# Channel mixers whose up panels keep tokens stationary, with results turned in 32x32 blocks

## The chip, the cores and the metric

The kernel runs on one core of one Trainium2 chip. A core has TensorE (PE in the profile) for matrix products, VectorE (DVE), ScalarE (ACT), GpSimd (POOL) and SyncE (SP), which only issues transfers, and 16 DMA engines. PE takes a stationary operand of 128x128 from SBUF, streams up to 512 columns of a moving operand past it and adds the product into a PSUM bank. The metric is the device time of one execution in microseconds, the median over runs.

## The reference

A decoder trunk of two layers works on 256 tokens of width 2048 in fp32. Each layer is a mixer (gated linear attention in the first, forgetting attention in the second, both with four heads of attention to 256 memory tokens) and then a channel mixer. The change touches only the channel mixer:

```python
def causal_dwconv(u, w, b):
    s_ = u.shape[1]
    up = jnp.pad(u, ((0, 0), (CONV_WIDTH - 1, 0), (0, 0)))
    return w[0] * up[:, 0:s_] + w[1] * up[:, 1:s_ + 1] + w[2] * up[:, 2:s_ + 2] + b

def conv_ffn(h, w_up, conv_w, conv_b, w_down):
    u = causal_dwconv(h @ w_up, conv_w, conv_b)
    a, val = split_cols(u, [FFN_HIDDEN, FFN_HIDDEN])
    return (jax.nn.silu(a) * val) @ w_down
...
h = rmsnorm(x, norm_ffn[i])
x = x + conv_ffn(h, ffn_w_up[i], ffn_conv_w[i], ffn_conv_b[i], ffn_w_down[i])
```

The hidden width is 5632, so `w_up` has 11264 columns (gate, then value). The convolution runs over the tokens, with three taps and a bias for each column.

## The kernel before, in words

**Numbers in halves.** PE works on `float32r`. Each fp32 operand is kept as a high half (a copy rounded to that type) and a low half (what the copy lost), and a product is three products: high by high, high by low, low by high. An activation buffer (`bufA`, `bufB`) is 16 tiles of 128 features x 2 halves x 256 tokens, features on the partitions. A norm's gain is folded into the halves; its factor for each token (`row()`) is multiplied in after the projection.

**Weights.** All weights lie in memory as a row of units of 1024 columns x 128 partitions (512 KB), in the order of use (`_panels`, `_layout`). `split_unit` (L189) loads a unit through SyncE (L200), makes the high half on ACT (L205) and the low half on DVE (L206). There are four buffers each for the raw unit, the high half and the low half. These instructions are traced with a priority 300 instructions ahead, so that they run as early as the buffers allow.

**Two forms of a projection.** With weights stationary (`proj_fm`, `panels_fm`, L240 and L242), a panel of 256 columns takes four units. For each chunk of 128 features and each 128 columns there is one matmul of 512 moving columns (high weights, both halves of the 256 tokens) and one of 256 (low weights, high tokens). Results come out with features on the partitions, as two partial sums that `whole` (L249) adds: a copy on ACT (L252) and an addition on DVE (L254). With tokens stationary (`proj_tm` L286, `panel_tm` L311), a panel of up to 512 columns takes eight units of two chunks. For each chunk and each block of 128 tokens there are three matmuls whose moving operand is the weights. Results come out with tokens on the partitions, already summed in PSUM.

**The channel mixer** (`ffn`, L1023). The 44 blocks of 128 hidden columns are done in three parts of 16, 16 and 12 (`PARTS`). For each part, all its up panels run first, then four down panels of 512 output columns that contract over the blocks of that part; the result is added to the residual `x` (L322). An up panel holds 128 gate and the matching 128 value columns, weights stationary. `up_out` brings each half of it through `whole`, multiplies by the norm's row (L1038), applies the convolution (ACT L1042 for one tap and the bias, DVE L1043 and L1044 for the others), then silu (L1047), the product (L1048) and the split into halves in `m` (L352, L353). The first three up panels of a layer are interleaved by `three_fm` so that their last units, which need the last four feature chunks of `h`, come late.

**Turning.** Where the residual has to become features on partitions for the next stage (`preparing`, L1062), DVE turns it in 32x32 blocks (L1077), and `move` (L462, L466) sends the blocks between partition groups by 16 DMAs of 32 KB on SyncE. `split_turned` then reads the moved tile (L363, L365).

**Order of the work.** A scheduler orders each engine's instructions when the program is built, by priority and by its own estimate of when they can start. The order on each engine is then fixed, and waits are by semaphore. `issue_after` holds instructions behind a given one on its engine. SyncE issues in order too: a load or move that must wait holds up those behind it.

**PSUM.** Eight banks: four for accumulators (`pacc`), and in `pwork` two under the tag `s` and one each under `t` and `o`.

Of the kernel before, what the change touches and what calls it, by code (L numbers as in the profile page):

```python
# [12 lines left out]
F32 = mybir.dt.float32  # L13
# [6 lines left out]
P = 128  # L20
# [3 lines left out]
HID = 5632  # L24
# [30 lines left out]
def _panels():  # L55
# [5 lines left out]

    def fm(key, w, c0, kcs=full, second=None):
        cols = [(c0, 256)] if second is None else [(c0, 128), (second, 128)]
        out.append((key, w, kcs, cols, 4))

# [75 lines left out]
def _trunk(ctx: ExitStack, tc: tile.TileContext, xt, xtok, memt, wp, wgu, gns, gfin, cnv, par, msk, out):  # L141
# [39 lines left out]

    loads, casts, ends = [], [], []

# [5 lines left out]
    def split_unit(unit, pool=wpool, pieces=1, before=None):  # L189

        off, kcs, n = unit
        w = len(kcs) * n
        with tc.high_priority(offset=AHEAD):
            raw = wpool.tile([P, NUNIT], F32, name="raw", tag="raw", bufs=4)
            hi = pool.tile([P, NUNIT], F32R, name="whi", tag="whi", bufs=4 if pool is wpool else 3)
            lo = pool.tile([P, NUNIT], F32R, name="wlo", tag="wlo", bufs=4 if pool is wpool else 3)
            src = wp[off : off + P * w].rearrange("(p n) -> p n", p=P)
            for i in range(pieces):
                s = slice(i * w // pieces, (i + 1) * w // pieces)
                loads.append(nc.sync.dma_start(raw[:, s], src[:, s]))  # L200
            for i in range(pieces):
                s = slice(i * w // pieces, (i + 1) * w // pieces)
                if before is not None:
                    before(i)
                casts.append(S.activation(hi[:, s], raw[:, s], AF.Copy))  # L205
                V.tensor_tensor(lo[:, s], raw[:, s], hi[:, s].bitcast(F32), ALU.subtract)  # L206
        return hi, lo
# [84 lines left out]

    def panel_tm(key, src, evac):

# [22 lines left out]

        return step

    def add_to(f):  # L320
# [692 lines left out]

    def add_out(key, src, then=None, spare=None, last=None, first=0):
        for f in range(first, 4):
            def evac(b, a, f=f):
                add_to(f)(b, a)
                if then is not None:
                    then(f, b)

            proj_tm((*key, f), src, last if f == 3 and last is not None else evac, spare if f == 3 else None)

    def ffn(l, nx, h, m, then, spare=None, last=None):  # L1023
        with tc.tile_pool(name=f"ffn{l}", bufs=1) as fp:
# [5 lines left out]
            turn = [0]  # L1030
            for p, (lo, hi) in enumerate(PARTS):
                def up_out(j, i):
                    cv = {}

                    def evac(c, a):
                        u = us[turn[0] % 4]
                        turn[0] += 1
                        V.tensor_tensor(u[:, 2:], whole(a), nx.row(), ALU.mult)  # L1038
# [4 lines left out]
                        V.scalar_tensor_tensor(r, u[:, 1 : T + 1], w[1], r, ALU.mult, ALU.add)  # L1043
                        V.scalar_tensor_tensor(r, u[:, :T], w[0], r, ALU.mult, ALU.add)  # L1044
                        cv[c] = r
                        if c == 1:
                            S.activation(cv[0], cv[0], AF.Silu)  # L1047
                            V.tensor_tensor(r, cv[0], r, ALU.mult)  # L1048
                            split(m, i, r)

                    return evac

                first = 0
# [45 lines left out]
    with tc.tile_pool(name="stash", bufs=1) as st:  # L1099
# [4 lines left out]
        with tc.tile_pool(name="turn1", bufs=1) as tp:  # L1104
            n2, then = preparing("kv", bufB, tp, turned3, "mix1")
            ffn(0, n, bufB, bufA, then)
        fox(n2, vt, turned3)
# [9 lines left out]
    with tc.tile_pool(name="store", bufs=1) as op:  # L1117
# [41 lines left out]

        ffn(1, n, bufA, bufB, then, op, last)  # L1160

# [70 lines left out]
```

## Time and profile before

| what | value |
|---|---|
| median of 3 runs | 2263.23 us (2262.76 to 2263.59) |
| the profiled execution's own time | 2263.27 us |
| its span in the trace | 2261.4 us |
| PE busy | 2249.8 us, 99% |
| DVE busy | 1617.1 us, 72% |
| ACT busy | 1250.7 us, 55% |
| granted PE clock | 0.999 |
| HBM over the span | 192 GB/s |

Engines are busy beside one another. PE's matmuls overlap in the records, so the mean length of one record (390 ns for 512 columns) is longer than the distance from one matmul to the next. The distance has to be taken from stretches of many. A group's idle time is what its engine stood just before its instructions, with what ended the wait; it costs time only on an engine that sets the end. "SPq" rows are the issuing of a DMA by SyncE, not its transfer.

### The profile page before, as it was taken

How to read it: one execution, taken by the hardware profiler on the slowest of the kernel's cores; microseconds unless marked ns; L12 is line 12 of the kernel's file. 1: busy time of each engine (PE TensorE's matmuls, PEld its weight loads, DVE VectorE, ACT ScalarE, POOL GpSimd, SP SyncE). 2: the span in 40 equal slices, each digit the busy share in tenths (PEclk: the TensorE clock that was granted, in tenths of full speed). 3: DMA queues.
4: the chain of work that ended last, by engine and by line, in shares of the span. 5: the costliest groups of instructions: out<-in, count | busy, mean ns of one | idle time of the engine just before them, and what ended most of it. 6: DMA issues, size and time to landing. Idle time of an engine off the chain costs nothing.

```text
span 2261.4 us, 33526 instructions
## 1 busy us (share of the span) xinstructions
PE 2249.8 (99%) x12253; PEld 1967.1 (87%) x12253; DVE 1617.1 (72%) x2746; ACT 1250.7 (55%) x1986; POOL 3.4 (0%) x19
## 2 busy tenths in 40 slices
PE   9999999999999999999999999999999999999998
PEld 8889998888888888888888998888888888888887
DVE  7779877677765777557777569677776577756775
ACT  6657675555543555445555555456554455534554
POOL 0000000000000000000000000000000000000000
PEclk9999999999999999999999999999999999999999
DMA  9655554665555555555565567766656555655554
GB/s 341 198 184 166 177 168 171 214 201 190 191 196 189 190 193 188 195 188 192 189 217 202 183 192 240 229 204 218 194 189 198 188 189 191 192 194 187 191 193 147
DMA packets 142125, 444.38 MB, mean 197 GB/s; under 512 B 18428, under 2 KB 34952, under 8 KB 141832
## 3 DMA queue, kind: packets, MB, share of 16 engines
q1 hardware_dynamic: 140808, 441.05, 58.8%
q8 instruction: 96, 1.57, 0.3%
q10 hardware_dynamic: 1152, 1.19, 0.2%
q14 instruction: 69, 0.57, 0.1%
HBM read 429.31 MB, written 5.52 MB: 192 GB/s over the span
## 4 chain that ended last, share of the span: by engine, by line
PE 96%; ACT 1%; DVE 1%; DMA 1%; issue 0%; SPq 0%; DVEq 0%; ACTq 0%
PE acc L242 37%; PE acc L286 34%; PE acc L240 20%; PE acc L311 2%; PE ps_s L242 1%; PE ps_s L240 1%; DMA raw<-wp 0%; ACT whi L205 0%; DVE wlo L206 0%; PE ps_s L758 0%; PE ps_o L495 0%; PE ps_s L495 0%; PE ps_o L931 0%; PE ps_s L976 0%; ACT L822 0%
## 5 line engine op out<-in xcount | busy, mean ns | idle before, releaser
L206 DVE TENSOR_TENSOR wlo<-raw,whi 128x1024 fp32r<-128x1024 f32 (+4 forms) x809 | 968.7, 1201 | 518.5 <-ACT whi L205 429.9
L205 ACT ACTIVATE whi<-raw 128x1024 fp32r<-128x1024 f32 (+4 forms) x809 | 839.6, 1039 | 600.5 <-PE acc L286 311.2
L242 PE MATMUL acc<-B,whi 128*128 128x512 f32 x2048 | 482.6, 390 | 0.0
L242 PEld LDWEIGHTS acc<-B,whi 128*128 128x128 f32 x2048 | 378.9, 188 | 75.2
L286 PE MATMUL acc<-whi,mix 128*128 128x512 f32 x1216 | 302.5, 389 | 0.0
L242 PE MATMUL acc<-mix,whi 128*128 128x512 f32 x1224 | 298.3, 391 | 0.0
L286 PEld LDWEIGHTS acc<-whi,mix 128*128 128x128 f32 x1216 | 228.3, 188 | 47.4
L242 PEld LDWEIGHTS acc<-mix,whi 128*128 128x128 f32 x1224 | 226.0, 188 | 44.4
L240 PEld LDWEIGHTS acc<-B,wlo 128*128 128x128 f32 x2048 | 255.7, 191 | 5.3
L240 PE MATMUL acc<-B,wlo 128*128 128x256 f32 x2048 | 259.4, 283 | 0.0
L286 PE MATMUL acc<-whi,B 128*128 128x512 f32 (+3 forms) x896 | 200.5, 360 | 0.0
L286 PEld LDWEIGHTS acc<-whi,B 128*128 128x128 f32 x896 | 162.7, 188 | 15.9 <-ACT whi L205 0.3
L286 PE MATMUL acc<-wlo,mix 128*128 128x512 f32 x608 | 164.5, 389 | 0.0
L240 PEld LDWEIGHTS acc<-mix,wlo 128*128 128x128 f32 x1224 | 154.9, 191 | 6.0 <-ACT mix L363 1.6
L240 PE MATMUL acc<-mix,wlo 128*128 128x256 f32 x1224 | 157.9, 284 | 1.2 <-ACT mix L363 1.2
L286 PEld LDWEIGHTS acc<-wlo,mix 128*128 128x128 f32 x608 | 114.1, 188 | 23.7
L242 PE MATMUL acc<-A,whi 128*128 128x512 f32 x536 | 131.3, 390 | 0.0
L252 ACT ACTIVATE part<-acc 128x256 f32<-128x256 f32 x238 | 89.4, 378 | 58.8 <-PE acc L242 58.8
L242 PEld LDWEIGHTS acc<-A,whi 128*128 128x128 f32 x536 | 100.1, 188 | 20.5
L286 PE MATMUL acc<-wlo,B 128*128 128x512 f32 (+3 forms) x448 | 111.6, 360 | 0.0
L1042 ACT ACTIVATE cv<-u,cw 128x256 f32<-128x256 f32 x176 | 104.2, 595 | 4.2 <-DVE u L1038 4.1
L352 ACT ACTIVATE mix<-cv 128x256 fp32r<-128x256 f32 x60 | 25.0, 416 | 143.6 <-DVE cv L1048 143.6
(250 smaller groups left out, 1809.4 us busy)
## 6 DMA issues: line engine op xcount, KB each, us to landing
raw<-wp SPq DMA_DIRECT2D x743, 512.0 KB, 3.8
raw<-wp SPq DMA_DIRECT2D x32, 384.0 KB, 3.1
raw<-wp SPq DMA_DIRECT2D x24, 388.0 KB, 3.5
turn<-blk SPq DMA_DIRECT2D x144, 32.0 KB, 3.0
raw<-wp SPq DMA_DIRECT2D x8, 400.0 KB, 3.0
far<-y SPq DMA_DIRECT2D x6, 384.0 KB, 6.1
z<-far SPq DMA_DIRECT2D x24, 96.0 KB, 2.9
xf<-xt SPq DMA_DIRECT2D x16, 128.0 KB, 5.2
```

The lines of the kernel that those rows point to most:

```text
L205: casts.append(S.activation(hi[:, s], raw[:, s], AF.Copy))
L206: V.tensor_tensor(lo[:, s], raw[:, s], hi[:, s].bitcast(F32), ALU.subtract)
L240: mm = TE.matmul(acc[p][c][:, :T], w[:, s], both[:, 0, :], start=False, stop=end and j == 3)
L242: mm = TE.matmul(acc[p][c], w[:, s], both, start=u == j == 0, stop=end and j == 3)
L252: S.activation(t, a[:, T:], AF.Copy)
L286: mm = TE.matmul(acc[b][:, :n], src[kcs[j] - base][:, part, b * P : (b + 1) * P], w, start=u == 0 and low == part == j == 0, stop=u == end ...
L311: mm = TE.matmul(acc[b][:, :n], src[kc - base][:, part, b * P : (b + 1) * P], ready[low][:, j * n : (j + 1) * n], start=i == low == part = ...
L352: S.activation(hi, src, AF.Copy)
L1042: S.activation(r, u[:, 2:], AF.Identity, bias=w[3], scale=w[2])
```

## The change

Two up panels become one. It holds 256 gate and 256 value columns and is computed with tokens stationary, in the form of the down panels: eight units of two chunks, 96 matmuls of 512 columns, in place of 2 x 64 of 512 and 256 columns.

- Results now have tokens on the partitions. As each token block is finished, DVE turns it out of PSUM in 32x32 blocks into a tile `y`. After the second block, `move` sends `y` to `z` with 16 DMAs on SyncE. `whole` is no longer used here.
- `convolve` does the rest as before for the two 128-column blocks of the panel, reading `z` in strided runs. It is not run at the panel's end. `close(1)`, after unit 1 of a later panel, convolves all finished panels but the newest, and `issue_after` holds the instructions on DVE behind the low half of that unit.
- The first two up panels of a layer are interleaved by `two_tm`: six units of each, then the last two units of each. The second of the two accumulates in the `s` banks.
- In every part the first two down panels are interleaved in the same way (all but the last two units of each, then the rest). During them the part's last two panels are convolved: after unit 1 of the first down panel and after unit 2 of the second.
- `y` and `z` use tiles that are free by then: in the first layer the tags `mk0` and `mv0`, and the three slices of the stash; in the second layer `mk0`, `mk1` and `mv0`, `mv1`.

```diff
         for p, (lo, hi) in enumerate(PARTS):
-            for j in range(lo, hi):
-                fm(("up", l, j), ("ffn_w_up", l), j * P, second=HID + j * P)
+            for j in range(lo, hi, 2):
+                tm(("up", l, j), ("ffn_w_up", l), j * P, 2 * P, more=[(HID + j * P, 2 * P)])
...
-                V.tensor_tensor(lo[:, s], raw[:, s], hi[:, s].bitcast(F32), ALU.subtract)
+                lows.append(V.tensor_tensor(lo[:, s], raw[:, s], hi[:, s].bitcast(F32), ALU.subtract))
...
-    def panel_tm(key, src, evac):
+    def panel_tm(key, src, evac, second=False):
...
-                acc.extend(pacc.tile([P, 512], F32, name="acc", tag="acc") for _ in range(2))
+                acc.extend(work("s", 2) if second else pacc.tile([P, 512], F32, name="acc", tag="acc")
+                           for _ in range(2))
...
+    def two_tm(steps, count, last, hooks={}):
+
+        for units in (range(count - last), range(count - last, count)):
+            for p, step in enumerate(steps):
+                for u in units:
+                    step(u)
+                    hooks.get((p, u), int)()
...
+        if hooks is not None:
+            first = 2
+            two_tm([panel_tm((*key, f), src, evac_of(f), second=f == 1) for f in range(2)],
+                   len(where[(*key, 0)]), 2, hooks)
+        for f in range(first, 4):
+            proj_tm((*key, f), src, last if f == 3 and last is not None else evac_of(f), spare if f == 3 else None)
...
-                    def evac(c, a):
+            def by_run(t):
+                return t.rearrange("p (b q j) -> p q b j", b=2, j=32)
+
+            def convolve(j, i, z):
+
+                for s in range(2):
+                    cv = {}
+                    for c in range(2):
                         u = us[turn[0] % 4]
                         turn[0] += 1
-                        V.tensor_tensor(u[:, 2:], whole(a), nx.row(), ALU.mult)
-                        col = (c * 44 + j) * 4
+                        V.tensor_tensor(by_run(u[:, 2:]), z[:, :, 2 * c + s], by_run(nx.row()), ALU.mult)
+                        col = (c * 44 + j + s) * 4
...
+            def up(j, i, second=False):
+
+                y, z = ys[count[0] % len(ys)], zs[count[0] % len(zs)]
+                count[0] += 1
+
+                def evac(b, a):
+                    V.transpose(y[:, :, :, b, :], a.rearrange("p (k c i) -> p c k i", c=4, i=32))
+                    if b:
+                        move(z, y)
+                        open_.append((j, i, z))
+
+                return panel_tm(("up", l, j), h, evac, second)
+
+            def close(left):
+
+                while len(open_) > left:
+                    with tc.issue_after(lows[-1].ins):
+                        convolve(*open_.pop(0))
+
             for p, (lo, hi) in enumerate(PARTS):
+                js = list(range(lo, hi, 2))
                 if p == 0:
-                    first = 3
-                    three_fm([("up", l, j) for j in range(3)], h, [up_out(j, j) for j in range(3)])
-                for j in range(lo + first, hi):
-                    proj_fm(("up", l, j), h, up_out(j, j - lo))
+                    two_tm([up(j, j - lo, j > lo) for j in js[:2]], 8, 2)
+                    js = js[2:]
+                for j in js:
+                    step = up(j, j - lo)
+                    for u in range(8):
+                        step(u)
+                        if u == 1:
+                            close(1)
                 end = p == len(PARTS) - 1
-                add_out(("down", l, p), m, then if end else None, spare if end else None, last if end else None)
+                down = {"then": then, "spare": spare, "last": last} if end else {}
+                add_out(("down", l, p), m, hooks={(0, 1): lambda: close(1), (1, 2): lambda: close(0)}, **down)
```

More of the change, by code (lines that the diff above doesn't have):

```diff
@@ L60, in _panels, with fm @@
     out = []
-    def fm(key, w, c0, kcs=full, second=None):
-        cols = [(c0, 256)] if second is None else [(c0, 128), (second, 128)]
-        out.append((key, w, kcs, cols, 4))
+    def fm(key, w, c0, kcs=full):
+        out.append((key, w, kcs, [(c0, 256)], 4))
     def tm(key, w, c0, n, kcs=full, more=()):
@@ L180, in _trunk @@
             TE.matmul(warm, bufB[KC - 1][:, 0, :P], bufB[KC - 1], start=i == 0, stop=i == WARM - 1)
-    loads, casts, ends = [], [], []
+    loads, casts, lows, ends = [], [], [], []
     def work(tag, bufs=1):
@@ L1011, in fox, with add_out, evac_of @@
                     steps[f](u)
-    def add_out(key, src, then=None, spare=None, last=None, first=0):
-        for f in range(first, 4):
-            def evac(b, a, f=f):
+    def add_out(key, src, then=None, spare=None, last=None, first=0, hooks=None):
+        def evac_of(f):
+            def evac(b, a):
                 add_to(f)(b, a)
@@ L1105, in _trunk @@
             n2, then = preparing("kv", bufB, tp, turned3, "mix1")
-            ffn(0, n, bufB, bufA, then)
+            ys = [const.tile([P, 4, 4, 2, 32], F32, name="yu", tag=tag) for tag in ("mk0", "mv0")]
+            ffn(0, n, bufB, bufA, ys, turned3, then)
         fox(n2, vt, turned3)
@@ L1158, in last @@
                 (nc.scalar if f == 1 else nc.sync).dma_start(out[b, :, f * 512 + lo : f * 512 + hi], t)
-        ffn(1, n, bufA, bufB, then, op, last)
+        ys, zs = ([const.tile([P, 4, 4, 2, 32], F32, name="yzu", tag=f"{t}{i}") for i in range(2)] for t in ("mk", "mv"))
+        ffn(1, n, bufA, bufB, ys, zs, then, op, last)
 def _constants():
```

19 lines of the change are left out of this document (9 added, 10 removed).

## The prediction

> **What bounds the kernel now.** I read the page first (busy time, then the chain), then the chain in order of time, then stretches of one stage each, then the waits of TensorE, and only after that the queues of the other engines around the change.
>
> From the page of the kernel before: the span, busy time and share of each engine, and the chain that ended last by engine and by line.
> ```profile
> span 2261.4 us, 33526 instructions
> PE 2249.8 (99%) x12253; PEld 1967.1 (87%) x12253; DVE 1617.1 (72%) x2746; ACT 1250.7 (55%) x1986; POOL 3.4 (0%) x19
> PE 96%; ACT 1%; DVE 1%; DMA 1%; issue 0%; SPq 0%; DVEq 0%; ACTq 0%
> ```
> The chain is matmuls almost everywhere. A busy PE alone would not say so, as matmuls are pipelined; the waits do. These are all waits of PE after its first instruction that reach half a microsecond (total, times, longest):
> ```profile
> PE acc L240 <- ACT mix L363: 1.2, 1, 1.2
> PE acc L286 <- ACT whi L205: 0.7, 1, 0.7
> ```
> So PE practically never stands still, and only two things can move the time: what its own stream costs, and a new wait put into it. The chain in order of time prices the stream. Columns are start, length, what; the rows stand for the second third of the first channel mixer, sixteen up panels and then four down panels.
> ```profile
> 730.33 3.83 PE acc L240 x32
> 734.16 7.28 PE acc L242 x32
> ...
> 897.03 3.83 PE acc L240 x32
> 904.52 87.04 PE acc L286 x384
> ```
> Between the first and the last L240 row lie 15 up panels: (897.03 - 730.33) / 15 = 11.113 us each, 64 matmuls: 32 of 512 columns and 32 of 256. The down panels are all of 512 columns with tokens stationary: 87.04 / 384 = 226.7 ns each, with no gap. Taking the same 226.7 ns for the 32 wide matmuls of an up panel (7.253 us), the 32 narrow ones take 3.86 us, 120.6 ns each. Two narrow ones therefore cost 241 ns, where one wide one costs 227.
>
> Stretches of one kind (PE, PEld, DVE and ACT busy, granted clock, DMA share, GB/s): sixteen up panels, then four down panels, then two pieces of the last third in which 32 KB moves run beside the matmuls.
> ```profile
> 727.00:905.00 178.00, 178.00 (x1026) 157.67 (x1025) 133.85 (x215) 100.82 (x156) 0.00 (x0) 1.00 0.56 189
> 905.00:992.00 87.00, 87.00 (x385) 72.06 (x384) 47.80 (x51) 36.40 (x38) 0.00 (x0) 1.00 0.57 196
> 1157.00:1174.00 17.00, 17.00 (x77) 14.08 (x76) 12.56 (x20) 10.10 (x21) 0.00 (x0) 1.00 0.67 216
> 1174.00:1190.00 16.00, 16.00 (x72) 13.27 (x71) 15.26 (x34) 12.02 (x25) 0.00 (x0) 1.00 0.68 225
> ```
> The clock is full in all four. DVE is the next engine, 75% busy in the up stage. The last row matters most for what follows: PE was busy for all 16 us while DVE was busy for 15.26 of 16.
>
> **The change, part by part.** *The matmul stream.* A pair of old up panels is 2 x 11.113 = 22.227 us. The new panel of 256 gate and 256 value columns is 16 chunks x 2 token blocks x 3 passes = 96 wide matmuls, the form of the down panels, so 96 x 226.7 ns = 21.760 us. Saved: 0.467 us a pair, and with 44 pairs in two layers **20.5 us**. Columns streamed and weight bytes loaded are equal; 32 starts a pair go away. This is on the path.
>
> Here a rule speaks against the sum. The Trainium skill ("TensorE: Matmul & The Clock Gate", section "Wait — 56ns, not 53.3ns?") gives a matmul at full clock its columns at 2.4 GHz plus about 2.5 ns; by it 32 starts fewer save 0.08 us a pair, 3.5 us in all. The rows give 13.3 ns beyond the columns for the wide form and about 14 for the narrow, so the trace disagrees and I keep 20.5.
>
> *DVE and ACT.* Groups by line and form, with count, busy time and mean in ns, then idle before:
> ```profile
> L206 DVE TENSOR_TENSOR wlo<-raw,whi 128x1024 fp32r<-128x1024 f32 x743 | 905.7, 1222 | 471.3 <-ACT whi L205 385.7 <-issue 52.0 <-PE acc L240 20.8
> L254 DVE TENSOR_TENSOR wholes<-acc,part 128x256 f32<-128x256 f32 x238 | 98.9, 418 | 1.0 <-ACT part L252 0.7
> L252 ACT ACTIVATE part<-acc 128x256 f32<-128x256 f32 x238 | 89.4, 378 | 58.8 <-PE acc L242 58.8
> L1038 DVE TENSOR_TENSOR u<-wholes,row 128x256 f32<-128x256 f32 x176 | 74.0, 423 | 2.7
> L1043 DVE SCALAR_TENSOR_TENSOR cv<-u,cw,cv 128x256 f32<-128x256 f32 x176 | 83.7, 478 | 0.0
> L1044 DVE SCALAR_TENSOR_TENSOR cv<-u,cw,cv 128x256 f32<-128x256 f32 x176 | 84.0, 480 | 0.1
> L1048 DVE TENSOR_TENSOR cv<-cv,cv 128x256 f32<-128x256 f32 x88 | 37.5, 426 | 8.7 <-ACT cv L1047 0.2
> L353 DVE TENSOR_TENSOR mix<-cv,mix 128x256 fp32r<-128x256 f32 x60 | 25.5, 424 | 24.7 <-ACT mix L352 24.7
> L1077 DVE STREAM_TRANSPOSE blk<-x 128x512 f32<-128x512 f32 x24 | 16.9, 706 | 3.7 <-DMA turn<-blk 3.3
> L365 DVE SCALAR_TENSOR_TENSOR B<-turn,gains,B 128x128 fp32r<-128x128 f32 x40 | 11.3, 347 | 3.9 <-ACT B L363 3.8
> ```
> A pair loses four additions of the halves (4 x 418 = 1.67 us of DVE) and four copies (4 x 378 = 1.51 us of ACT), and gains two transposes of 128x512 (2 x 706 = 1.41 us). Transposes out of PSUM are not in the trace; L254 reads PSUM at 418 ns where L1038 needs 423 from SBUF, so I take the SBUF price; if PSUM cost as much again, 1.4 us more. The multiplication by the row of the norm now reads runs of 32 or 64: L365 reads such a block at 347 ns for 128 elements, near the price of plain forms of that length, so nothing is added. DVE goes from 133.85 / 8 = 16.73 us a pair to about 16.5 in 21.76 (76%), ACT from 12.6 to 11.1 (51%). Both stay hidden as long as no wait stops them; the room on DVE is 5.3 us a panel, and the last stretch above shows PE undisturbed with far less.
>
> *The moves.* Every panel issues 16 SyncE DMAs of 32 KB, 704 in all, in the queue that loads the weights. The same move exists at L466 in the last third. SyncE's issue time (ns min/median/max), the time to landing, and the first and last rows of one such move among the loads (start, length), with ACT's first read of what landed:
> ```profile
> L466 SPq DMA_DIRECT2D fvt<-blk x48: 507/583/1073, 1143.9 to 1188.1; - x48
> DMA to landing us min/median/max: 1.8/2.9/6.4
> 1124.92 65.28 PE acc L286 x288
> 1159.06 1.15 SPq L466 DMA_DIRECT2D fvt<-blk  x2
> 1160.30 0.53 SPq L200 DMA_DIRECT2D raw<-wp  x1
> ...
> 1171.97 1.78 SPq L466 DMA_DIRECT2D fvt<-blk  x3
> 1175.73 1.71 ACT L363 ACTIVATE B<-fvt,gains 128x256 fp32r<-128x256 f32 x4 [1.00 <-DMA fvt<-blk]
> ```
> Sixteen moves are 16 x 0.583 = 9.3 us of SyncE, eight loads 8 x 0.53 = 4.2: 13.6 of 21.76, so the queue has room. A load can be late by one whole move at most, 9.3 us; four raw buffers and three prepared units stand before PE, each unit 12 x 226.7 ns = 2.72 us, which is 19 us of cover. I take nothing; without the cover it would be up to 6.6 us a panel (9.3 less one unit). DMA engines go from 0.56 to about 0.67 of their time, as in the last two stretches. The down panel in these rows ended on PE at 1124.92 + 144 x 0.2267 = 1157.56, so its turned block was read 18.2 us after its last matmul.
>
> *The new wait.* Inside a part, a panel's convolution is queued on DVE behind the low half of unit 1 two panels on. PE takes that unit 21.76 + 2.72 = 24.5 us after the panel's end; DVE may make it three units (8.2 us) sooner, at about 16.3 to 17.5. The block is there at about 18.2, so DVE may stand 1 to 2 us, with the next low halves queued behind. Inside the 5.3 us of room and the three prepared units that costs nothing.
>
> *The ends of the parts.* The last two panels are now convolved during the down panels, whose last two units wait for them. One old convolution during down panels (DVE rows, first and last step, start and length):
> ```profile
> 640.62 0.43 DVE L1038 TENSOR_TENSOR u<-wholes,row 128x256 f32<-128x256 f32 x1
> 649.24 0.42 DVE L353 TENSOR_TENSOR A<-cv,A 128x256 fp32r<-128x256 f32 x1
> ```
> That is 9.0 us for one hidden block. Two blocks that share DVE need 7.2 us of DVE work (4 x (0.423 + 0.478 + 0.480) from lines L1038, L1043, L1044, and 2 x (0.426 + 0.424) from L1048 and L353) beside low halves taking 1.22 of each 2.72 us, so 10 to 13 us. In the first two parts the last panel is wanted 13 units, 35.4 us, after its end; 18.2 + 13 = 31.2 is in time. In the last part there are six units a panel, and it is wanted after 9 units, 24.5 us: late by 4 to 6.7 us unless PE finds other work. The other panel's unit 4 is such work (2.72 us), and the third down panel after it. I take 1.5 us a layer, **+3.0**; the ends are 0 and 6.7 a layer.
>
> *The head of a layer.* Only the second layer's head stalls now; PE's wait of 1.2 us above is this one (PE, then ACT, with the wait in brackets):
> ```profile
> 1522.89 3.79 PE L242 MATMUL acc<-mix,whi 128*128 128x512 f32 x16
> 1530.94 0.50 PE L240 MATMUL acc<-mix,wlo 128*128 128x256 f32 x2 [1.19 <-ACT mix L363]
> 1530.38 1.71 ACT L363 ACTIVATE mix<-turn,gains 128x256 fp32r<-128x256 f32 x4 [4.33 <-DMA turn<-blk]
> ```
> The new order wants chunk 8 after four units, 10.9 us after the head's start at 1522.9, so at 1533.8, when those splits have run: **-1.2**; between 0 and -1.2. Chunks 12 to 15 are wanted after 12 units (32.6 us) instead of nine (25): safer. The down panels' new order costs PE nothing: same matmuls.
>
> *Sum*, against the profiled execution's own 2263.27 us (span 2261.4 and 1.9 around it; the median of the runs is 2263.23, the same within 0.04): 2263.27 - 20.5 - 1.2 + 3.0 = **2244.6 us**, 0.8% faster. This case's own range is 2240 (no late convolution, both small waits gone) to 2252.
>
> **The rivals.** *Late hand-over, nothing fills it.* The last part's convolution costs its full 6.7 us in both layers, and the 1.2 us stays: 2263.3 - 20.5 + 13.4 = 2256.2. For it: the block is read 18.2 us late by a row, and nothing shortens that. Against: PE's order is written with such waits in view, and there are units to put in between.
>
> *No gain.* A narrow matmul costs just half a wide one where weights stream, 113.3 instead of 120.6 ns; then the pair saves nothing and the time is about 2262 to 2266. The 15 panels in a row speak against it. The skill's figure above would land here too, at 2261.6.
>
> *Slower: DVE stands at the turned block in every panel.* Its price begins when the wait exceeds 5.3 us, and beyond 5.3 + 0.47 = 5.8 us the kernel is slower: the block would have to arrive some 22.5 us after the panel's end instead of 18.2. This is possible, since the transposes queue behind the previous convolution on a DVE that is 76% busy (around the move shown it was 74%, 12.56 of 17, but in smaller pieces), and one move can issue at 1.07 us. Each microsecond beyond costs 32 us over the 32 panels that are convolved between other up panels; half a microsecond beyond gives 2263.3 + 16 = 2279. Against it: 4.3 us of margin, and a move whose pace is set by loads that keep the same rate.
>
> **How the numbers follow.** My forecast has 0.64, the late hand-over (with smaller losses of that kind) 0.16, no gain 0.05, slower 0.15. Within 0.2% (4.5 us, about what a measurement of this kernel can tell from no change) is 2258.7 to 2267.8. So faster 0.80, same 0.05, slower 0.15. The predicted time is the forecast's; the range runs from 2240 to 2259, which takes in the late hand-over at 2256 and leaves out 0.2.
>
> **What would show it.** In the changed kernel, pieces of 96 matmuls of 21.76 us in the up stage, PE's waits inside the parts still near zero, DVE about 76% busy there, SyncE issuing 704 more DMAs of near 0.58 us, and DMA share near 0.67. Wrong would be: PE waiting for the low half in every panel with DVE behind the moves (slower), PE waiting for the mixer's products at the ends of the last parts by more than 3 us each (the sum's term), or wide matmuls of over 231 ns in the up stage (no gain).

## The result, and the profile after

The changed kernel takes 2297.12 us (median of 4 runs, 2294.28 to 2303.18) beside 2263.41 us of the kernel before on the same chip. The ratio is 1.015, with a 95% interval of 1.0129 to 1.0172: it is 1.5% slower, where 0.8% faster was forecast. The profiled execution took 2296.63 us.

Three lines of the page of the changed kernel: span, busy time and share of each engine, and the chain that ended last by engine.
```profile
span 2294.8 us, 31197 instructions
...
PE 2246.3 (98%) x10845; PEld 1896.0 (83%) x10845; DVE 1585.4 (69%) x2658; ACT 1202.3 (52%) x1810; POOL 3.4 (0%) x19
...
PE 20%; DVE 5%; DMA 5%; issue 1%; SPq 1%; ACT 1%; DVEq 0%; ACTq 0%
```
TensorE's busy time fell from 2249.8 to 2246.3 us, and the span rose by 33.4. So the time lies in gaps. The chain, 96% matmuls before, now names other engines: VectorE, the DMAs and SyncE have 5, 5 and 1% of the span. (It could be followed back only to 1561.7 us, so all its shares together cover a third of the span.) PE's waits that add up to a microsecond or more (total, times, longest) say who it stands for:
```profile
PE acc L313 <- DVE wlo L205: 17.3, 17, 1.7
PE ps_s L313 <- DVE wlo L205: 8.9, 7, 2.6
PE acc L241 <- DVE ny L426: 4.4, 1, 4.4
PE acc L285 <- ACT whi L204: 3.5, 2, 1.8
PE acc L239 <- ACT B L373: 2.8, 1, 2.8
PE ps_o L179 <- DVE B L176: 1.4, 1, 1.4
```
The first two rows are 26.2 us of waiting for the low half of a weight unit, which VectorE makes, in units of L313, that is of the up panels and the first two down panels of a part. The third and the fifth lie at the head of the forgetting attention, right behind the first channel mixer.

To see which stages lost, I divide each trace at the same nine places of the stream of weight matmuls (the starts of the same matmuls, counted by columns streamed). All entries are us; the rows below the second are experiments told further down.

| kernel | before 1st mixer | 1st mixer: part 1 | part 2 | part 3 | head of the attention | to 2nd mixer | 2nd mixer: part 1 | part 2 | part 3 | rest |
|---|---|---|---|---|---|---|---|---|---|---|
| before | 461.39 | 265.15 | 264.85 | 198.64 | 66.97 | 265.89 | 266.66 | 264.85 | 198.68 | 8.36 |
| changed | 460.93 | 268.81 | 267.11 | 206.67 | 76.85 | 265.99 | 268.96 | 265.11 | 205.34 | 9.06 |
| late4 | 460.13 | 261.39 | 261.12 | 195.84 | 77.28 | 265.71 | 262.11 | 261.12 | 195.89 | 9.07 |
| late4_y0 | 460.43 | 261.39 | 261.12 | 195.84 | 67.53 | 265.71 | 262.14 | 261.12 | 195.89 | 9.06 |

Against the last row, which is the change without its waits, the changed kernel loses 7.4 + 6.0 + 10.8 us in the first mixer, 9.3 at the head of the attention, and 6.8 + 4.0 + 9.5 in the second mixer, 53.8 of the 54.6 us between the two spans. The loss is spread over the parts; it isn't an event at one place.

One round on VectorE, from its timeline in the changed kernel (start, length, what; in brackets the idle time before it): the convolution's first step (L1062, two blocks of gate and value) and the two transposes of the next panel out of PSUM (L1080).
```profile
595.20 1.43 DVE L1062 TENSOR_TENSOR u<-fvt,row 128x256 f32<-128x256 f32 x4 [5.19 <-DMA raw<-wp]
598.47 0.71 DVE L1080 STREAM_TRANSPOSE yu<-acc 128x512 f32<-128x512 f32 x1
600.65 0.71 DVE L1080 STREAM_TRANSPOSE yu<-acc 128x512 f32<-128x512 f32 x1
619.67 1.44 DVE L1062 TENSOR_TENSOR u<-fvt,row 128x256 f32<-128x256 f32 x4 [5.71 <-DMA raw<-wp]
622.95 0.71 DVE L1080 STREAM_TRANSPOSE yu<-acc 128x512 f32<-128x512 f32 x1
624.74 0.71 DVE L1080 STREAM_TRANSPOSE yu<-acc 128x512 f32<-128x512 f32 x1
```
TensorE's rows of the same stretch: the end of a panel, and one stall.
```profile
591.30 0.62 PE L313 MATMUL acc<-wlo,B 128*128 128x512 f32 x2
591.75 1.98 PE L313 MATMUL acc<-whi,B 128*128 128x512 f32 x8
...
622.30 1.20 PE L313 MATMUL acc<-wlo,B 128*128 128x512 f32 x4 [0.44 <-DVE wlo L205]
```
And the issuing of the moves on SyncE between the two convolutions, its first and last rows:
```profile
601.39 1.15 SPq L476 DMA_DIRECT2D fvt<-yu  x2
...
614.58 0.51 SPq L476 DMA_DIRECT2D fvt<-yu  x1
```
Read them as a circle. The panel ended on TensorE at 591.75, but VectorE stood at the block of the panel before until 595.20, and this panel's transposes are queued behind that convolution: the second one ended at 601.36, 9.6 us after the panel. Then its 16 moves went out, between 601.39 and 615.09, and its convolution could start at 619.67, 18.3 us after the transposes. VectorE had stood 5.71 us for it, so the next panel's transposes ended at 625.45, 5.8 us after 619.67, late again. One turn is 18.3 + 5.8 = 24.1 us, and a panel's matmuls take 21.76. (The releaser in brackets is inferred, and by the code the convolution reads no weights. The last move's issue and the median 3.8 us to landing of these moves give 618.9, within 0.8 us of the start. The experiment "ready", which takes only this dependence away, settles that it is the moved block.) That circle was my theory. The rival was that the 704 extra DMAs delay the weight loads themselves, so that VectorE has nothing to make low halves from.

### The profile page after: what moved, and what is told of

Same layout as the page of the kernel before. It is cut to its first block, busy times and chain, and to the rows that moved or that the text cites. A ratio compares the mean times of both kernels' runs of the same rounds, so it can differ in the third digit from the quotient of the medians.

```text
span 2294.8 us, 31197 instructions
## 1 busy us (share of the span) xinstructions
PE 2246.3 (98%) x10845; PEld 1896.0 (83%) x10845; DVE 1585.4 (69%) x2658; ACT 1202.3 (52%) x1810; POOL 3.4 (0%) x19
## 5 line engine op out<-in xcount | busy, mean ns | idle before, releaser
L313 PE MATMUL acc<-whi,B 128*128 128x512 f32 x1488 | 373.9, 390 | 0.0
L313 PEld LDWEIGHTS acc<-whi,B 128*128 128x128 f32 x1488 | 279.1, 188 | 58.1 <-ACT whi L204 0.2
L313 PE MATMUL acc<-whi,mix 128*128 128x512 f32 x1312 | 325.7, 390 | 0.0
L313 PEld LDWEIGHTS acc<-whi,mix 128*128 128x128 f32 x1312 | 246.3, 188 | 51.5 <-ACT whi L204 0.3
L313 PE MATMUL acc<-wlo,B 128*128 128x512 f32 x744 | 203.9, 390 | 6.4 <-DVE wlo L205 6.3
L285 PE MATMUL acc<-whi,mix 128*128 128x512 f32 x736 | 187.6, 395 | 3.5 <-ACT whi L204 3.5
L313 PE MATMUL acc<-wlo,mix 128*128 128x512 f32 x656 | 177.8, 392 | 10.9 <-DVE wlo L205 10.9
L313 PEld LDWEIGHTS acc<-wlo,B 128*128 128x128 f32 x744 | 139.1, 188 | 37.9 <-DVE wlo L205 9.3
L241 PE MATMUL acc<-B,whi 128*128 128x512 f32 x672 | 164.2, 394 | 4.4 <-DVE ny L426 4.4
L285 PEld LDWEIGHTS acc<-whi,mix 128*128 128x128 f32 x736 | 140.1, 191 | 33.7 <-ACT whi L204 4.4
L285 PE MATMUL acc<-whi,B 128*128 128x384 f32 (+3 forms) x736 | 160.0, 354 | 0.0
L313 PEld LDWEIGHTS acc<-wlo,mix 128*128 128x128 f32 x656 | 122.2, 188 | 40.5 <-DVE wlo L205 15.8
L241 PEld LDWEIGHTS acc<-B,whi 128*128 128x128 f32 x672 | 123.9, 189 | 28.7 <-ACT mix L373 4.8
L285 PEld LDWEIGHTS acc<-whi,B 128*128 128x128 f32 x736 | 132.7, 188 | 9.7 <-ACT whi L204 0.3
L313 PE MATMUL acc<-whi,A 128*128 128x512 f32 x368 | 94.6, 389 | 0.0
L239 PE MATMUL acc<-B,wlo 128*128 128x256 f32 x672 | 88.0, 284 | 2.8 <-ACT B L373 2.8
L239 PEld LDWEIGHTS acc<-B,wlo 128*128 128x128 f32 x672 | 85.1, 191 | 5.2 <-ACT B L373 3.2
```

The costliest lines, as they stand in the source:

```text
L239: mm = TE.matmul(acc[p][c][:, :T], w[:, s], both[:, 0, :], start=False, stop=end and j == 3)
L241: mm = TE.matmul(acc[p][c], w[:, s], both, start=u == j == 0, stop=end and j == 3)
L285: mm = TE.matmul(acc[b][:, :n], src[kcs[j] - base][:, part, b * P : (b + 1) * P], w, start=u == 0 and low == part == j == 0, stop=u == end ...
L313: mm = TE.matmul(acc[b][:, :n], src[kc - base][:, part, b * P : (b + 1) * P], ready[low][:, j * n : (j + 1) * n], start=i == low == part = ...
```

## The experiments

Each edit is to the changed kernel. Ratios are to the kernel before.

**late4** closes a panel inside the parts behind unit 4 of the next one instead of unit 1. All DMAs stay.
```diff
-                        if u == 1:
+                        if u == 4:
                             close(1)
```


> The only edit: inside the parts a panel is convolved behind the low half of unit 4 of a later panel instead of unit 1. Every move, matmul and DVE instruction stays. The loop theory: in the changed kernel DVE reaches the convolution 13 us after the previous panel's second transpose, the turned block is there after 18, and the next panel's transposes stand behind that wait, so one round takes 18 + 6 = 24 us where a panel's matmuls take 21.76. Three units (8.2 us) later the block is there and the next transposes are already done: DVE's waits of 4 to 6 us at the multiplication vanish inside the parts, the period of the transposes falls to 21.8, the sixteen-block stages lose 4 to 7 us each, and the time falls by 22 to 28 us to about 2272. The queue theory (704 more DMAs in SyncE's queue make weight loads late, and PE lacks weights): the moves are all still there, so the time stays at 2297 within 5 us.

2251.68 us (2250.4 to 2254.38), ratio 0.9948 (0.9933 to 0.9963). One window from the start of the first mixer on (length, then PE, PEld, DVE, ACT and POOL busy, granted clock, DMA share, GB/s), the changed kernel's first and late4's second:
```profile
461.00:1100.00 639.00, 629.15 (x2763) 516.75 (x2762) 427.42 (x628) 310.59 (x397) 0.00 (x0) 1.00 0.65 204
```
```profile
461.00:1100.00 639.00, 639.00 (x2821) 529.30 (x2821) 443.01 (x640) 318.16 (x405) 0.00 (x0) 1.00 0.64 211
```
TensorE is busy for all 639 us again, at the same load of the DMA engines. VectorE's rows in the stretch above:
```profile
589.82 0.71 DVE L1080 STREAM_TRANSPOSE yu<-acc 128x512 f32<-128x512 f32 x1
591.16 0.72 DVE L1080 STREAM_TRANSPOSE yu<-acc 128x512 f32<-128x512 f32 x1 [0.64 <-PE acc L313]
...
595.21 1.43 DVE L1062 TENSOR_TENSOR u<-fvt,row 128x256 f32<-128x256 f32 x4
...
611.58 0.71 DVE L1080 STREAM_TRANSPOSE yu<-acc 128x512 f32<-128x512 f32 x1
```
The transposes now stand ahead of the convolution and wait for TensorE alone. The convolution waits for nothing, and the period is 611.58 - 589.82 = 21.76 us. It moved the time by 45 us, with the same transfers: the rival's late loads fall. I had expected about 2272, 20 us more than came out, because I took the last parts' losses for something else; the table shows that parts 3 were the same circle (206.67 to 195.84). Apart from the 1.4 us of L179, which stood in the changed kernel too, the only waits of PE of over half a microsecond that are left are the two at the head of the attention:
```profile
PE acc L241 <- DVE ny L426: 4.2, 1, 4.2
PE acc L239 <- ACT B L373: 2.8, 1, 2.8
```

**late2** takes unit 2, one unit later than the change.
```diff
-                        if u == 1:
+                        if u == 2:
                             close(1)
```


> As the run with unit 4, but unit 2: the convolution comes one unit (2.7 us) later than in the changed kernel. The loop theory: DVE's wait at the block shrinks from about 5 to about 2.5 us, but the next transposes still stand behind it, so the round stays above 21.76 and only part of the loss goes: 2282 to 2294. If the wait alone cost time, not the round, half the loss inside the parts would go (about 2284). The queue theory: 2297 within 5 us.

2252.45 us (2251.82 to 2254.6), ratio 0.9952 (0.9937 to 0.9967): all of late4's gain. I had expected a part of it. VectorE's rows:
```profile
569.85 1.43 DVE L1062 TENSOR_TENSOR u<-fvt,row 128x256 f32<-128x256 f32 x4
571.20 0.71 DVE L1080 STREAM_TRANSPOSE yu<-acc 128x512 f32<-128x512 f32 x1
...
572.19 0.71 DVE L1080 STREAM_TRANSPOSE yu<-acc 128x512 f32<-128x512 f32 x1
...
591.61 1.43 DVE L1062 TENSOR_TENSOR u<-fvt,row 128x256 f32<-128x256 f32 x4
592.96 0.71 DVE L1080 STREAM_TRANSPOSE yu<-acc 128x512 f32<-128x512 f32 x1
```
Here the transposes still come right behind a convolution's start, so standing there isn't the fault by itself. VectorE comes for each block one unit later, finds it, and parts 1 and 2 of the first mixer take 261.39 and 261.12 us, what they take in late4. But the edit does a second thing. The scheduler now puts both transposes closer behind the convolution's start: the second one ends 572.19 + 0.71 - 569.85 = 3.1 us after it, instead of 5.8. With 18.3 us for the move, that turn would be 21.4 us, under the 21.76 of a panel, where my expectation kept it above. The run doesn't tell whether the later coming or the shorter turn did it; by the circle either is enough.

**late0** takes unit 0, one unit earlier, to put the circle against a plain wait in every panel, which would cost a whole unit more each time.
```diff
-                        if u == 1:
+                        if u == 0:
                             close(1)
```


> The changed kernel with the convolution one unit earlier still, behind unit 0, the opposite direction. If each panel simply pays for the time by which DVE comes too early, one unit (2.72 us) more for each of 32 panels would add up to 87 us: 2340 to 2385. The loop theory: DVE's wait grows to about 8 us, but the round from one second transpose to the next is still 18 us of move plus some 6 us of DVE steps, so the period stays at 23.5 to 24.5 us; only the onset comes about one panel earlier in each part: 2297 to 2313.

2301.46 us (2300.87 to 2305.03), ratio 1.0174 (1.0157 to 1.0191), 4.3 us above the changed kernel, where a plain wait was put at 2340 to 2385. VectorE's rows:
```profile
595.64 1.43 DVE L1062 TENSOR_TENSOR u<-fvt,row 128x256 f32<-128x256 f32 x4 [3.64 <-DMA fvt<-yu]
601.11 0.70 DVE L1080 STREAM_TRANSPOSE yu<-acc 128x512 f32<-128x512 f32 x1
...
624.63 0.71 DVE L1080 STREAM_TRANSPOSE yu<-acc 128x512 f32<-128x512 f32 x1
```
The turn is 624.63 - 601.11 = 23.5 us, near the 24.1 of the changed kernel, though VectorE was asked to come a unit earlier. Once it paces the stage, the turn is set by the move and the steps behind it, not by when VectorE asks. VectorE's wait at the block, which I had expected to grow to about 8 us, is 3.64 us here. The releaser named is the move itself.

**ready** lets the convolution read the tile before the move. All moves are still issued, but nobody waits for them. It leaves out the exchange between partition groups: the values come from blocks that still lie in the wrong ones.
```diff
-                        open_.append((j, i, z))
+                        open_.append((j, i, y))
```


> The convolution reads the transposed but unmoved block y instead of z; all 704 moves are still issued and land in z, which nothing reads. The hidden values are computed from misplaced blocks, that is what is left out. The loop theory: no wait for a landing is left in the channel mixer, neither inside the parts nor at their ends, so the inner loss (22 to 28 us) and the last parts' late products (some 7 us each with the halved clock behind them) go: 2255 to 2262, with only the forgetting attention's head still late by about 10 us. The queue theory: the same transfers in the same queue, 2297 within 5 us.

2243.46 us (2243.14 to 2243.87), ratio 0.991 (0.9896 to 0.9925). VectorE's rows, then TensorE's end of that panel, then SyncE's first and last row of its move, then the time to landing in the groups of DMA issues:
```profile
571.86 0.71 DVE L1080 STREAM_TRANSPOSE yu<-acc 128x512 f32<-128x512 f32 x1
587.92 1.43 DVE L1062 TENSOR_TENSOR u<-yu,row 128x256 f32<-128x256 f32 x4
```
```profile
569.62 0.61 PE L313 MATMUL acc<-wlo,B 128*128 128x512 f32 x2
```
```profile
572.59 1.15 SPq L476 DMA_DIRECT2D fvt<-yu  x2
...
585.74 0.51 SPq L476 DMA_DIRECT2D fvt<-yu  x1
```
```profile
fvt<-yu SPq DMA_DIRECT2D x352, 32.0 KB, 3.6
```
This is the circle at rest, and shows how small its cause is. The last of the panel's matmuls are those from 569.62, so it ended at about 570.1. The transposes ended at 572.57 (2.5 us later, behind the convolution before), and the move landed at about 585.74 + 0.51 + 3.6 = 589.9. VectorE came at 587.92. A block that is 2 us late is all it takes; fed back through the transposes, it grows until the turn paces the stage. I had expected the head of the attention to stay late, at 2255 to 2262. It came back too (67.18), which I had not understood then; late4_y0 takes it up.

**actq** leaves the convolution behind unit 1 and issues 8 of the panel's 16 moves from ScalarE's queue.
```diff
-                        move(z, y)
+                        move(z, y, lambda q, c: c > 1)
```


> The changed kernel with the convolution still behind unit 1; of the 16 moves of an up panel, eight (two of the four source column groups) are issued from ACT's queue instead of SyncE's. ACT pays 8 x 0.59 = 4.7 us a panel for it and is half idle. The loop theory: the block lands some 9 to 11 us after the second transpose instead of 18, before DVE reaches the convolution at 13 to 15, so no wait arises, the round is below 21.76 and the inner loss goes as in the runs with the later convolution; the last part's products come earlier too: 2245 to 2256. If the order on DVE (transposes behind the convolution) costs time by itself, whatever the landing, the time stays near 2290.

2252.93 us (2250.43 to 2254.12), ratio 0.9953 (0.9938 to 0.9968). The circle is broken from its other side. VectorE's rows:
```profile
834.38 0.70 DVE L1080 STREAM_TRANSPOSE yu<-acc 128x512 f32<-128x512 f32 x1
...
850.44 1.43 DVE L1062 TENSOR_TENSOR u<-fvt,row 128x256 f32<-128x256 f32 x4
```
VectorE comes 15.4 us after the transposes, as in ready, and now starts without a wait, so the block is there by then. That is closer than I had expected (9 to 11 us after the transposes); the last section looks at the two queues.

**oldlast** has the last part of each mixer in the old form (single panels, weights stationary, down panels in sequence); the first two parts are as changed. The old `up_out` comes back for this; the core of the edit is
```diff
-            for j in range(lo, hi, 2):
+            mid = lo + 0 if p == len(PARTS) - 1 else hi
+            for j in range(mid, hi):
+                fm(("up", l, j), ("ffn_w_up", l), j * P, second=HID + j * P)
+            for j in range(lo, mid, 2):
```


> The last part of each channel mixer (12 blocks) has its old form: weights stationary, twelve panels, down panels in sequence; the first two parts are as changed. The trace of the changed kernel puts 8.0 us over the old time in the first layer's last part, 9.9 in the head of the forgetting attention behind it, and 6.7 in the second layer's last part. If these three are made by the last part's new order (late products there; and two down panels ending together, so that their 32 moves, then the next 32, queue up on SyncE ahead of the attention's first chunks), all three go: 2297 - 24.6 = 2272, and the head of the attention is back at 67 us. If the attention's head is late for another reason, 2282.

2270.55 us (2267.86 to 2272.73, 7 runs), ratio 1.0032 (1.0021 to 1.0044), as expected. Parts 3 return to 198.64 and 198.68, the head to 66.97, and the first two parts lose as in the changed kernel (266.46 and 268.19 in the first mixer).

So the head's 10 us come from the last part's new form, even where no circle runs (late4: 77.28). Its stall starts at the residual. The head's first matmuls need the new residual turned and moved by SyncE, four times 16 DMAs in order. VectorE's rows of late4 there, the first two down panels added to `x`, then two of the turns:
```profile
1147.63 1.37 DVE L332 TENSOR_TENSOR x<-x,acc 128x512 f32<-128x512 f32 x2 [2.12 <-PE acc L313]
1149.54 0.65 DVE L332 TENSOR_TENSOR x<-x,ps_s 128x512 f32<-128x512 f32 x1
...
1169.31 1.30 DVE L1123 STREAM_TRANSPOSE blk<-x 128x512 f32<-128x512 f32 x2 [2.54 <-DMA fvt<-blk]
...
1184.07 1.30 DVE L1123 STREAM_TRANSPOSE blk<-x 128x512 f32<-128x512 f32 x2 [2.41 <-DMA fvt<-blk]
```
The two panels end together, where the old order had them a panel apart, and the first move begins at 1152.0 instead of 1143.9. From then on the four moves queue one behind the other: in late4 they run 1152.0 to 1166.5, 1166.6 to 1179.8, 1180.5 to 1197.0 and 1201.0 to 1212.0, where those of the kernel before ended at 1203.5. Four experiments asked what makes them late.

**late4_kvact**: late4, with half of these moves issued from ScalarE's queue.
```diff
-                move(z, y)
+                move(z, y, lambda q, c: name == "kv" and c > 1)
```


> Convolution behind unit 4 as before, and in the first layer's last part half of the 64 moves that prepare the forgetting attention's keys and values are issued from ACT. In the run with unit 4 the first two down panels end 4 us apart, their moves queue one behind the other on SyncE until the attention's head has begun, PE waits there for 4.4 and 2.9 us and runs 6.8 us at half clock: 10.7 us. If SyncE's queue is the cause, these vanish: 2251.7 - 10.7 = 2241. If the cause is the late end of the two panels themselves, at most half of it goes: 2246 to 2252.

2252.96 us (2252.26 to 2255.06), ratio 0.9956 (0.9941 to 0.9971): no gain, and above both of my expectations; the head is at 77.31. It doesn't settle the point, because the first move was no faster. SyncE's eight went out from 1152.6 to 1168.2, 15.6 us, where all sixteen took 14.5 in late4. ScalarE's eight were out by 1161.5. Between 1150 and 1170 SyncE stood 7.7 us at weight loads that waited for VectorE (5.4 in late4).

**late4_mix**: late4, where the last part has 8 blocks in the new form, then 4 in the old form, and down panels in sequence.
```diff
-            for j in range(lo, hi, 2):
+            mid = lo + 8 if p == len(PARTS) - 1 else hi
+            for j in range(lo, mid, 2):
...
+            for j in range(mid, hi):
+                fm(("up", l, j), ("ffn_w_up", l), j * P, second=HID + j * P)
```


> Convolution behind unit 4 as before; in each layer's last part only eight of the twelve blocks have the new form, the last four have the old one (weights stationary), and its four down panels run in sequence as before the change. No product is late and no two down panels end together, so the head of the attention loses nothing: 2251.7 - 10.7 + 4 x 0.467 = 2242.9. If the head's 10.7 us have another cause than the order of the last part: 2253 to 2254.

2249.43 us (2247.68 to 2250.92), ratio 0.9939 (0.9924 to 0.9954), 6.5 us above what I expected. The head fell only to 71.84, and PE waited 3.1 us for the high half of a weight unit on ScalarE. Why is open.

**late4_y0**: late4, where in one place, the last panel of the first mixer, the convolution reads the tile before the move, as in ready. The interleaved down panels and all else stay. It leaves out the exchange between partition groups for that panel.
```diff
-                        open_.append((j, i, z))
+                        open_.append((j, i, y if (l, j) == (0, 42) else z))
```


> Convolution behind unit 4; one panel of the 44, the last one of the first layer, is convolved from the unmoved block y, so its products do not wait for its move (the values of that one panel are computed from misplaced blocks, that is what is left out; all moves are still issued). Theory of the late products: that panel's wait holds up the first two down panels, they end together and 7 us late, their moves run into the attention's head and cost it 10.7 us; without the wait they end apart and the loss goes: 2241 to 2244. Theory of the interleaved order: the two down panels are still interleaved and their moves still queue up, so the loss stays: 2250 to 2253.

2242.26 us (2242.01 to 2243.24), ratio 0.9908 (0.9895 to 0.9922). The head is back at 67.53. VectorE adds the first two down panels to `x` at
```profile
1139.76 0.69 DVE L332 TENSOR_TENSOR x<-x,acc 128x512 f32<-128x512 f32 x1
...
1145.28 0.68 DVE L332 TENSOR_TENSOR x<-x,ps_s 128x512 f32<-128x512 f32 x1
```
The first comes 7.9 us sooner than in late4 and 5.5 us ahead of the second. The convolution of that last panel starts at 1123.23, where late4 has it at 1133.31 behind a wait of 2.17 us for its block; the rest of the 10 us is the earlier place that it now has on VectorE. So it isn't the interleaving as such: it is the late products of the part's last panel, for which the first two down panels wait. TensorE fills the time with other units and loses nothing in the part, but the residual is late, the moves that it starts are late, and the next stage pays 9.75 us.

**late4_old0**: late4, with the old form in the last part of the first mixer alone.
```diff
-            for j in range(lo, hi, 2):
+            mid = lo if p == len(PARTS) - 1 and l == 0 else hi
+            for j in range(mid, hi):
+                fm(("up", l, j), ("ffn_w_up", l), j * P, second=HID + j * P)
+            for j in range(lo, mid, 2):
```


> Convolution behind unit 4; only the first layer's last part has the old form (weights stationary, down panels in sequence), the second layer is new throughout. With the last part's new order gone where a head follows, the attention's head should lose nothing and the half-clock stretch there should be gone: 2251.7 - 10.7 + 6 x 0.467 = 2243.8. If the head's loss has another cause, 2254.

2244.98 us (2244.8 to 2245.62, 5 runs), ratio 0.9919 (0.9906 to 0.9933). It is faster than the kernel before by 0.8%, and than the changed one by 2.3% (2244.98 / 2297.12 = 0.977). All PE waits after the first instruction that its trace shows from 0.3 us on:
```profile
PE ps_o L183 <- DVE B L180: 1.4, 1, 1.4
PE ps_s L772 <- ACT later L820: 0.5, 1, 0.5
PE ps_s L317 <- ACT whi L208: 0.3, 1, 0.3
```

## Why the prediction was wrong

**The new wait** is the step that failed. It put VectorE at the block 16.3 to 17.5 us after the panel's end, the block there at 18.2, and a wait of 1 to 2 us; ready shows 17.8, 19.8 and 2.0. The numbers were near enough. The sentence "Inside the 5.3 us of room and the three prepared units that costs nothing" was wrong. Room in VectorE's busy time covers a wait only if nothing that VectorE does behind it starts the next wait. Here the next panel's transposes stand behind it, and these start the next move. The step listed the low halves as queued behind the convolution and left the transposes out; only the rival below named them. I should have summed the turn (18.3 + 5.8 = 24.1 us) and held it against 21.76.

**The rival "DVE stands at the turned block in every panel"** named the place, and the queue behind the previous convolution as a reason, but its condition and price were wrong. It wanted the block 22.5 us after the panel's end from outside; the circle itself took it from 19.8 to 27.9 (619.67 - 591.75). It priced 32 us for each further microsecond, which would be over 170. In fact the stage settles at the turn's pace, 1.4 to 2.3 us over a panel's matmuls, and a part of eight panels loses 4 to 7.4 us. The loss goes with the turn: in the second parts the second transposes of the first and the eighth panel start at 751.70 and 916.15 in the first mixer (23.5 us a panel, 6.0 lost), and at 1837.29 and 1999.55 in the second (23.2 us, 4.0 lost). That a part doesn't lose eight times the excess I put down to the first rounds of each part, which the prepared units absorb; no run separates that. The 4.3 us of margin that I held against this rival were not there.

**The moves** "I take nothing": as cost of issue and bandwidth that held. The DMA share (0.65, where about 0.67 was worked out) and 18 us a move came near, and late4 runs all 704 with no stall inside the parts. As latency they are three quarters of the turn.

**The matmul stream**, -20.5: exact where nothing waits. Parts 1 and 2 of the first mixer fall by 3.76 and 3.73 us in late4 (8 x 0.467 = 3.74), part 3 by 2.80 (6 x 0.467). The chain of the changed kernel has the same price in a stretch without waits:
```profile
1815.49 102.47 PE acc L313 x452
```
That is 226.7 ns a matmul, in the up stage of the second mixer. The rival of no gain and the rule that spoke for it fall with these savings.

**DVE and ACT**: the transposes out of PSUM cost what those out of SBUF do. The group by line and form:
```profile
L1080 DVE STREAM_TRANSPOSE yu<-acc 128x512 f32<-128x512 f32 x42 | 29.7, 709 | 1.9 <-PE acc L313 1.9
```
709 ns beside 706.

**The ends of the parts**, +3.0: within the parts this was 0 (195.84 and 195.89, what the stream alone gives). TensorE found other units, as I had weighed. But the same lateness came out at another place, which the step didn't look at: the head of the attention, +10. **"The down panels' new order costs PE nothing"** missed it too; the matmuls are the same, but the order is what lets the late products hold up the first two residual tiles at once. A late hand-over was in the rivals, 13.4 us for two layers, but under the wrong stage.

**The head of a layer**, -1.2: the second mixer's part 1 falls by 4.55 us in late4, 3.74 of it stream, so -0.8.

Without its two waits the change comes near the sum. With nothing for the ends of the parts the sum is 2241.6, and late4_y0 took 2242.26, ready 2243.46. That late4_old0 took 2244.98, beside the 2244.6 of the forecast, is chance: it gives up 2.8 us of the stream where the sum had 3.0 for the ends. Of the 53.8 us that the table puts between the changed kernel and late4_y0, 44.5 lie within the parts and 9.3 at the head; 10.2 at most are the clock, below, and the rest are gaps.

Open: why the turn is shorter in the second mixer's second part with the same work, and the wait on ScalarE in late4_mix.

## What to carry to other kernels

Where a result leaves an engine, travels, and comes back to the same in-order engine, add up the whole turn: the travel time, and the engine's steps from the wait to the instruction that starts the next journey. If that exceeds the time that the bounding engine has for one round, the turn sets the pace, whatever the engine's busy share. Buffers seem to cover only the first rounds. Placing the waiting step one unit (2.7 us) later, which also brought the transposes closer behind it, was worth 45 us. And products that come late at the end of a stage, with the bounding engine still busy, can be paid for in the next stage's first transfer, 9.75 us here.

## What the runs showed of the hardware

**Short waits at a high price.** Windows of the changed kernel at three places (length, then PE, PEld, DVE, ACT and POOL busy, granted clock, DMA share, GB/s):
```profile
1161.80:1168.40 6.60, 5.92 (x14) 4.71 (x15) 5.56 (x10) 3.78 (x6) 0.00 (x0) 0.50 0.56 169
1209.60:1216.20 6.60, 4.50 (x11) 3.57 (x12) 6.07 (x27) 3.76 (x9) 0.00 (x0) 0.50 0.43 118
2243.80:2250.40 6.60, 5.51 (x13) 4.36 (x14) 5.97 (x11) 4.18 (x7) 0.00 (x0) 0.50 0.59 179
```
The clock was granted at one half for 6.83 us each time: at two waits of 2.5 and 1.8 us close together, at one of 4.4, and at two of 2.6 and 1.8. One wait of 2.8 us, at 1239, brought none. The kernel before has no such stretch but at its very end, and late4 has one, at the head. Three times half of 6.83 is 10.2 us. That is the most they can cost; TensorE was busy for 15.9 us in the three windows, and half of that is 8.0. So it is under a fifth of the 52 us by which the forecast missed, and my sum had no term for it. The Trainium skill ("TensorE: Matmul & The Clock Gate", Part 1, "The HAM clock gate") says that the gate knows half and full only and looks at activity in windows of 3413 ns; the trace agrees, as 6.83 us are two such windows.

**Two queues aren't twice as fast.** With half of a panel's moves on ScalarE's queue (actq), the last of SyncE's went out 12.7 us after the transposes (845.98 + 1.78 - 835.08); with all sixteen on SyncE (ready) it was 13.7 (585.74 + 0.51 - 572.57). The last rows of the two queues in actq, SyncE's, then ScalarE's:
```profile
845.98 1.78 SPq L476 DMA_DIRECT2D fvt<-yu  x3
842.72 1.16 ACTq L476 DMA_DIRECT2D fvt<-yu  x2
```
ScalarE's half, among its casts, was out at 843.88; SyncE's half ended last, at 847.76. Between 835 and 848 SyncE stood 3.0 us at weight loads that waited for VectorE and 1.3 us at moves that waited for a load to land; in ready, between 572 and 588, it stood 0.7 us at such loads and at no move for a landing. late4_kvact shows the same at another place. Why the loads wait longer there is open.
